# Mixer input stage of a two-layer hybrid decoder step: order of the projections, tiles of the samples' pages, first use of PSUM banks, second key layer

## Chip, cores and metric

The kernel runs on one core of a Trainium2 chip. The metric is the device time of one execution in microseconds (us), lower is better. TensorE (PE) does the matrix products, VectorE (DVE), ScalarE (ACT) and GpSimd (POOL) the element-wise work, SyncE (SP) issues most DMAs; POOL issues the indirect ones. Each engine takes its instructions in one fixed order that the planner wrote down at build time.

## What is computed

The reference runs two layers over 512 prompt tokens and 8 sample tokens (520 columns together). One layer is, cut to what matters here:

```python
x = LN(ALPHA*x + 0.5*swiglu_1(x))
z = x @ w_in                       # u | q | kc vc ks vs kw vw | NSA gates (24) | conv | merge gates
q, ks, kw = rope(q), rope(ks), rope(kw)
kc = gelu(windows(kc_all) @ phi_k1 + pe) @ phi_k2 ; kc = rope(kc)   # the compression branch
vc = gelu(windows(vc_all) @ phi_v1 + pe) @ phi_v2
y_b = g0*attend(q, kc, vc) + g1*attend(q, chosen blocks of ks, vs) + g2*attend(q, kw, vw)   # NSA
x = LN(ALPHA*x + (sig*P_A(s5) + sig*P_B(y_b) + sig*P_C(conv)) @ w_o)
x = LN(ALPHA*x + 0.5*swiglu_2(x))
```

For the 8 samples the rows of `kc`, `vc`, `ks`, `vs` of 2048 past positions lie in pages of 128 rows that a page table names (16 pages of each cache for each sample and layer), and `kw`, `vw` of 512 past positions in a window cache.

## The kernel before, in words

Each large product is done as three products of rounded halves (`mm3`, L239 to L241): 128 weight columns against 264 and then 256 of the 520 token columns, 8 steps of 128 rows, so 48 matmuls for one 128-column block. The weights arrive raw by DMA (`load_raw`, L218, two buffers `raw`) and are split into a rounded part on ACT (L228) and a rest on DVE or POOL (L229) (`split`, four buffers each of `whi` and `wlo`).

`mid` runs the mixers of a layer. It opens PSUM banks (4 `acc`, 2 `aux`, 2 `saT`) and calls `project_kvq`:

- The four blocks of q are computed first, first half of the columns for all four, then the second half, while the norm of the step before delivers its columns block by block (`norm`, L314 to L323).
- Then come kc, vc, ks, vs, kw, vw and the 24 gate columns, in that order, with transposes of finished blocks (`to_rows` L826 and L829, `q_back`, `k_back` L897 and L900) and rope on DVE between them.
- At its start it asks for the 16 compression pages of sample 0 (`fetch_cmp`, L641), for the selection pages of samples 0 and 1 (`fetch_sel`: 32 pages in four tiles of 8 pages, in each tile 3 by indirect DMA of POOL, L1118, and 5 by SP, L1122) and for two window tiles (`fetch_win`, L1127). The planner issues a DMA when its buffer is free, so what SP has queued decides when weights arrive.
- At the end the gates are transposed and spread (L936, L945), after `k_back` of kw.

Then `mid` closes the banks, opens one `saM`, two `saS`, two `cacc`, one `ctp`, and `compress_start` loads and splits the first-layer weights `phi_k1`, `phi_v1` (rest on POOL). `compress_cache` works on one sample at a time: eight steps (`prepare` L688 to L694, `products` L708, 12 matmuls a step, steps alternate between keys and values), then `second`: GELU, the second layer (keys: four matmuls with 64 weight columns each, `w2` and the rotated `w2r`, for two heads, L736; values L740) and the rope of keys (L742 to L744). Keys and values of one sample share a bank, which a matmul of zeros clears first (L702); sample 0 has a bank for each.

`samples` attends for two samples at a time (four groups g). Its scores and values are computed in quarters of the array, 32 columns each: L1189 (selection scores, two banks), L1198 and L1199 (window), L1249 (selection values), L1258 (window values), L1262 to L1264 (own row and compressed values). After the selection values of g it asks for the pages of g+1 into the same four tiles. The groups 0 to 2 are woven with two samples of `compress_cache` each, group 3 with the prompt's attention (`weave` takes the streams' next pieces by costs written in the code; the planner then moves single instructions ahead when it believes them ready).

Of the kernel before, what the change touches and what calls it, by code (L numbers as in the profile page):

```python
# [17 lines left out]
NTOK = 520  # L18
# [104 lines left out]
class Trunk:  # L123
# [36 lines left out]
    def make_consts(self):  # L160
# [7 lines left out]
        zero = c.tile([128, 16], BF, name="zero")  # L168
        nc.vector.memset(zero, 0.0)
        self.zerob = zero[:, 0:1].to_broadcast([128, 128])  # L170
# [329 lines left out]
    def mid(self, l):  # L500
# [16 lines left out]
        self.w2r = a.tile([128, 64], F32, name="w2r")  # L517
        self.hpe = a.tile([128, 2], F32, name="hpe")
        kcv, sag = self.pool(att, "kcv", 2, side="right"), self.pool(att, "sag", 4, side="right")
# [3 lines left out]
        self.open_banks(4, 2)  # L523
# [6 lines left out]
        with ExitStack() as sc, ExitStack() as pb:  # L530
            self.cacc, self.ctp = self.psum(pb, "cacc", 2), self.psum(pb, "ctp", 1)
            cp = self.pool(sc, "cmp")
            with ExitStack() as s0:
                C = self.compress_cache(l, cp, kcv, cx, G, self.compress_start(l, self.pool(s0, "cp")))
# [78 lines left out]
    def page_rows(self):  # L613
# [5 lines left out]
        with self.tc.tile_pool(name="pg", bufs=1) as p:  # L619
            f = p.tile([128, NS, 2, NG], F32, name="f")  # L620
            nc.vector.tensor_copy(f, self.pt.rearrange("p b (z n) -> p b z n", z=2)[:, :, :, :NG])
# [22 lines left out]
    def compress_start(self, l, p):  # L644

        nc, I = self.nc, self.I
        self.w1 = []
        pet = p.tile([128, 2, 2, 8], F32, name="pet")
        for i in range(2):
            raw = self.rawp.tile([128, 8, 256], F32, name="raw")  # L650
            w = raw.rearrange("p k (z h) -> p (k z) h", h=128)
            nc.sync.dma_start(w, I[("nsa_phi_k1", "nsa_phi_v1")[i]][l].rearrange("(q p) h -> p q h", p=128))
            nc.sync.dma_start(self.w2[:, i], I[("nsa_phi_k2", "nsa_phi_v2")[i]][l])
            nc.sync.dma_start(pet[:, i], I[("nsa_pe_k", "nsa_pe_v")[i]][l].rearrange("p (z q) -> p z q", z=2))
# [4 lines left out]
        nc.vector.memset(self.w2r, 0.0)  # L659
        nc.vector.tensor_scalar(self.w2r[:, 0:8], self.w2[:, 0, 8:16], -1.0, None, op0=OP.mult)  # L660
        nc.vector.tensor_copy(self.w2r[:, 8:16], self.w2[:, 0, 0:8])
        return p, pet

    def compress_cache(self, l, p, kcv, cx, G, start):
# [3 lines left out]
        p0, pet = start  # L668
# [5 lines left out]
        def prepare(b, G, s):  # L674

            qq, i = s // 2, s % 2
# [19 lines left out]
        def products(b, acc, s):  # L696
            qq, i = s // 2, s % 2
# [3 lines left out]
            if s == 0 and b:  # L701
                nc.tensor.matmul(acc[0], self.zerob, self.zerob[:, None, :].to_broadcast([128, 4, 128]), start=True,  # L702
                                 stop=False, skip_group_check=True)
            for m, x in enumerate((xh, xh, xl)):
                for q2 in range(2):
                    for z in range(2):
                        w = self.w1[i][z][m == 1]
                        nc.tensor.matmul(o, w[:, 2 * qq + q2, :], x[:, 2 * q2:2 * q2 + 2, z:z + n],  # L708
                                         start=not b and s < 2 and q2 + z + m == 0, stop=s > 5 and q2 == 1 and z == 1 and m == 2,
                                         skip_group_check=True)  # L710

        def second(b, acc):
# [20 lines left out]
            for j, w in enumerate((self.w2[:, 0], self.w2r)):  # L733
                for kv in range(2):
                    r = slice(kv * 64, kv * 64 + 64)
                    nc.tensor.matmul(pa[r, j * 128:j * 128 + 128], w, h[:, kv, :], start=True, stop=True)  # L736
                    if b == 0:
                        nc.tensor.matmul(pa[r, 384 + j * 32:416 + j * 32], w, hp[0][:, 0, kv], start=True, stop=True)
# [1216 lines left out]
```

## Time and profile before

| | us |
|---|---|
| median of 3 runs | 3106.2 (3099.05 to 3106.55) |
| profiled execution, its own time | 3104.94 |
| its span | 3103.2 |
| PE busy | 3028.1 (98%) |
| DVE busy | 1598.7 (52%) |
| ACT busy | 1120.1 (36%) |
| POOL busy | 536.1 (17%) |
| mean granted clock of PE | 0.987 |

The mean granted clock is a share of 2.4 GHz; a stretch with 0.50 runs at 1.2 GHz. Matmuls overlap, so a duration of one (0.28 us) is longer than the distance between two (0.12 us); a stretch's cost is read from starts. Layer 0's `project_kvq` begins about 403 us into the span and layer 1's about 1942 us; the stretch from there to the prompt's attention is the one that the change touches.

### The profile page before, as it was taken

To read this page: it belongs to the slowest core of one execution; us is meant where nothing else is said; L and a number is where in the kernel's file an instruction comes from. 1 tells how busy PE (TensorE), PEld (TensorE's weight loads), DVE (VectorE), ACT (ScalarE), POOL (GpSimd) and SP (SyncE) were. 2 spreads that over 40 slices of the span, in tenths; PEclk is the share of its full clock that TensorE was granted. 3 is DMA by queue.
4 is the path that set the end of the run, shared out by engine and by line. 5 is a ranking of instruction groups with operands and counts; after the bars stand their busy time and mean duration, and the time that the engine had idled before them with its cause. 6 is when DMAs were issued, how large, how long until landed. Compare 5 with 4: busy or idle time off the path is not lost. (4 is left out here: it accounts for less than half of the span.)

```text
span 3103.2 us, 62136 instructions
## 1 busy us (share of the span) xinstructions
PE 3028.1 (98%) x25364; PEld 2906.8 (94%) x25364; DVE 1598.7 (52%) x3586; ACT 1120.1 (36%) x2226; POOL 536.1 (17%) x809
## 2 busy tenths in 40 slices
PE   8999999999999999999999999999999999999998
PEld 8999998777999999999999999887789999999998
DVE  7633356566655365333496333565666453743334
ACT  4332235456224233232233222354652242333322
POOL 2611031321001021001147010213210010210010
PEclk9999999999999999999999999999999999999999
DMA  5543254632553232232234332547234433223221
GB/s 159 198 148 133 89 159 134 209 96 63 156 138 103 88 101 91 82 99 86 82 121 169 96 103 76 172 124 218 83 93 140 122 98 102 89 82 103 89 87 64
DMA packets 358630, 360.17 MB, mean 116 GB/s; under 512 B 40068, under 2 KB 341668, under 8 KB 358216
## 3 DMA queue, kind: packets, MB, share of 16 engines
q1 hardware_dynamic: 342584, 333.58, 34.4%
q0 software_dynamic: 7440, 20.00, 2.2%
q8 instruction: 199, 3.26, 0.4%
q10 hardware_dynamic: 8320, 2.62, 0.4%
q14 instruction: 87, 0.71, 0.1%
HBM read 332.48 MB, written 36.28 MB: 119 GB/s over the span
## 5 line engine op out<-in xcount | busy, mean ns | idle before, releaser
L239 PE MATMUL ps<-xh,whi 128*128 128x264 f32 (+1 forms) x4448 | 1257.6, 285 | 14.1 <-ACT whi L228 6.1
L240 PE MATMUL ps<-xl,whi 128*128 128x264 f32 (+1 forms) x4448 | 1257.4, 284 | 2.0 <-DVE xl L323 2.0
L241 PE MATMUL ps<-xh,wlo 128*128 128x264 f32 (+1 forms) x4448 | 1254.1, 283 | 2.4 <-DVE wlo L229 2.4
L229 DVE TENSOR_TENSOR wlo<-raw,whi 128x1024 fp32r<-128x1024 f32 (+3 forms) x432 | 496.0, 1151 | 741.2 <-ACT whi L228 736.9
L239 PEld LDWEIGHTS ps<-xh,whi 128*128 128x128 f32 x4448 | 837.2, 189 | 18.7 <-ACT whi L228 6.9
L240 PEld LDWEIGHTS ps<-xl,whi 128*128 128x128 f32 x4448 | 839.5, 189 | 3.5 <-DVE xl L323 2.2
L241 PEld LDWEIGHTS ps<-xh,wlo 128*128 128x128 f32 x4448 | 838.5, 189 | 4.1 <-DVE wlo L229 3.6
L228 ACT ACTIVATE whi<-raw 128x1024 fp32r<-128x1024 f32 (+2 forms) x452 | 444.6, 988 | 891.0 <-PE ps L240 776.4
L240 PE MATMUL ps<-hl,whi 128*128 128x256 f32 (+1 forms) x1408 | 398.3, 283 | 0.0
L239 PE MATMUL ps<-hh,whi 128*128 128x256 f32 (+1 forms) x1408 | 398.2, 283 | 0.0
L241 PE MATMUL ps<-hh,wlo 128*128 128x256 f32 (+1 forms) x1408 | 398.1, 283 | 0.0
L241 PEld LDWEIGHTS ps<-hh,wlo 128*128 128x128 f32 x1408 | 265.3, 188 | 0.2
L239 PEld LDWEIGHTS ps<-hh,whi 128*128 128x128 f32 x1408 | 264.9, 188 | 0.3
L240 PEld LDWEIGHTS ps<-hl,whi 128*128 128x128 f32 x1408 | 264.8, 188 | 0.1
L260 POOL TENSOR_TENSOR xf<-xf,shift 128x264 f32<-128x264 f32 (+1 forms) x84 | 79.4, 983 | 1028.6 <-ACT shift L257 1028.6
L384 DVE TENSOR_TENSOR s<-s,ps 128x264 f32<-128x264 f32 (+1 forms) x176 | 74.3, 424 | 277.3 <-PE ps L241 277.0
L708 PE MATMUL ps<-xc,whi 128*128 128x256 f32 (+1 forms) x1024 | 167.4, 297 | 1.0 <-ACT xc L693 0.9
L385 ACT ACTIVATE hh<-s 128x264 fp32r<-128x264 f32 (+1 forms) x176 | 72.7, 415 | 245.2 <-DVE s L384 245.1
L708 PEld LDWEIGHTS ps<-xc,whi 128*128 128x128 f32 x1024 | 142.2, 193 | 14.6 <-issue 7.7
L1118 POOL DMA_INDIRECT sg<-in_selT_dram,idx x96 | 96.2, 1002 | 275.9 <-PE ps L1249 248.7
L382 ACT ACTIVATE s<-ps 128x264 f32<-128x264 f32 (+1 forms) x176 | 66.3, 379 | 128.7 <-PE ps L241 126.5
L386 DVE TENSOR_TENSOR hl<-s,hh 128x264 fp32r<-128x264 f32 (+1 forms) x176 | 76.5, 436 | 33.5 <-ACT hh L385 33.5
(471 smaller groups left out, 4206.8 us busy)
## 6 DMA issues: line engine op xcount, KB each, us to landing
raw<-in_ffn_w_gu_dram SPq DMA_DIRECT2D x86, 1024.0 KB, 5.3
raw<-in_w_in_dram SPq DMA_DIRECT2D x38, 1024.0 KB, 5.4
raw<-in_ffn_w_down_dram SPq DMA_DIRECT2D x32, 1024.0 KB, 4.9
sg<-in_selT_dram SPq DMA_DIRECT2D x160, 128.0 KB, 3.1
cx<-in_cmpT_dram SPq DMA_DIRECT2D x128, 128.0 KB, 2.2
raw<-in_cmpT_dram SPq DMA_DIRECT2D x128, 128.0 KB, 2.5
raw<-in_ffn_w_down_dram SPq DMA_DIRECT2D x16, 768.0 KB, 4.3
W<-in_winT_dram SPq DMA_DIRECT2D x16, 512.0 KB
```

Of the source, the lines that this page charges most:

```text
L228: self.copy = self.nc.scalar.activation(hi, raw, AF.Copy)
L229: self.lo.tensor_sub(lo, raw, hi.bitcast(F32))
L239: nc.tensor.matmul(o, hi[:, k], rh, start=start and k == 0, stop=False)
L240: nc.tensor.matmul(o, hi[:, k], rl, start=False, stop=False)
L241: nc.tensor.matmul(o, lo[:, k], rh, start=False, stop=stop and k == nk - 1)
L260: nc.gpsimd.tensor_sub(self.xf[:, g, a:b], self.xf[:, g, a:b], sc[:, :n])
L382: nc.scalar.activation(s[:, :n], g, AF.Silu)
L384: nc.vector.tensor_mul(s[:, :n], s[:, :n], u)
L385: nc.scalar.activation(hh[:, j, a:b], s[:, :n], AF.Copy)
L386: nc.vector.tensor_sub(hl[:, j, a:b], s[:, :n], hh[:, j, a:b].bitcast(F32))
L708: nc.tensor.matmul(o, w[:, 2 * qq + q2, :], x[:, 2 * q2:2 * q2 + 2, z:z + n], start=not b and s < 2 and q2 + z + m == 0, stop=s > 5 and q2 ...
L1118: nc.gpsimd.indirect_dma_start(out=t[:, k], out_offset=None, in_=flat, in_offset=bass.IndirectOffsetOnAxis(ap=self.idx[:, l, b, z, k:k + 1 ...
```

## The change

- `project_kvq`: the order of the blocks is now q, kc, vc, ks, kw, gates, vs, vw. ks and kw share one raw buffer, vs and vw another, each filled by two DMAs of 128 columns (`kvq_tiles`); the gates' weights have a tile of their own, loaded early. The selection pages' SP DMAs of group 0 are queued behind the loads of all these weights (`rows_in`).
- The gates' transposes and spreading come before the last block; `phi_k1` is loaded and split before vw's product, `phi_v1` after it, rests on DVE (`compress_weights`); small weights come early (`compress_small`). The row outputs leave by POOL's queue.
- One compression bank (`cacc0`) is open during the projections, and `acc` has three banks there, not four.
- `compress_cache` does the four key steps first and then the four value steps; a `start` on the first matmul of each takes the place of the matmul of zeros. The second key layer is one matmul with 128 weight columns (`w2k`, plain and rotated side by side) over both heads; its rope is four multiplies on 64 partitions where two on 128 stood.
- The samples' pages lie in eight tiles of 4 pages; a group's first halves are asked for after half of the selection values of the group before, the second halves after all.
- Each bank of `samples` is opened by a DVE memset of its first column. The own-row and compressed values are ordered so that neighbours use different quarters.

```diff
@@ mid
-        self.open_banks(4, 2)
+        pb = ExitStack()
+        self.banks.close()
+        self.cacc = [self.psum(pb, "cacc0", 1)]
+        self.open_banks(3, 2)
...
-        with ExitStack() as sc, ExitStack() as pb:
-            self.cacc, self.ctp = self.psum(pb, "cacc", 2), self.psum(pb, "ctp", 1)
+        with ExitStack() as sc, pb:
+            self.cacc.append(self.psum(pb, "cacc1", 1))
+            self.ctp = self.psum(pb, "ctp", 1)
@@ compress_start / compress_weights
-            self.lo = nc.gpsimd
-            with self.tc.issue_after(self.queries.ins):
-                self.w1.append([self.split(w[:, 8 * z:8 * z + 8]) for z in range(2)])
-            self.lo = nc.vector
+    def compress_weights(self, l, i):
+        raw = self.rawp.tile([128, 8, 256], F32, name="raw")
+        w = raw.rearrange("p k (z h) -> p (k z) h", h=128)
+        self.nc.sync.dma_start(w, self.I[("nsa_phi_k1", "nsa_phi_v1")[i]][l].rearrange("(q p) h -> p q h", p=128))
+        self.w1.append([self.split(w[:, 8 * z:8 * z + 8]) for z in range(2)])
@@ compress_cache
-            qq, i = s // 2, s % 2
+            i, qq = s // 4, s % 4
...
-            if s == 0 and b:
-                nc.tensor.matmul(acc[0], self.zerob, self.zerob[:, None, :].to_broadcast([128, 4, 128]), start=True,
-                                 stop=False, skip_group_check=True)
...
-                                         start=not b and s < 2 and q2 + z + m == 0, stop=s > 5 and q2 == 1 and z == 1 and m == 2,
+                                         start=qq + q2 + z + m == 0, stop=qq == 3 and q2 == 1 and z == 1 and m == 2,
...
-            for j, w in enumerate((self.w2[:, 0], self.w2r)):
-                for kv in range(2):
-                    r = slice(kv * 64, kv * 64 + 64)
-                    nc.tensor.matmul(pa[r, j * 128:j * 128 + 128], w, h[:, kv, :], start=True, stop=True)
+            nc.tensor.matmul(pa[:, :256].rearrange("p (k n) -> p k n", k=2), self.w2k, h[:, 0:2, :], start=True, stop=True)
...
-            nc.vector.tensor_mul(t, pa[:, 128:256], self.C["kc_sin"])
-            nc.vector.tensor_mul(kcT, pa[:, :128], self.C["kc_cos"])
+            for kv in range(2):
+                r = slice(kv * 64, kv * 64 + 64)
+                nc.vector.tensor_mul(t[r], pa[64:128, kv * 128:kv * 128 + 128], self.C["kc_sin"][r])
+                nc.vector.tensor_mul(kcT[r], pa[0:64, kv * 128:kv * 128 + 128], self.C["kc_cos"][r])
@@ kvq_tiles (new)
+        yield from self.win_tiles(l, 512, 768)
+        for c in (0, 128):
+            if c:
+                yield self.split(self.graw)
+            raw = self.rawp.tile([128, 8, 256], F32, name="raw")
+            for i in range(2):
+                o = 1280 + c + 256 * i
+                self.rows_in = self.nc.sync.dma_start(raw[:, :, 128 * i:128 * i + 128],
+                                                      w[:, o:o + 128].rearrange("(k p) f -> p k f", p=128))
+            for i in range(2):
+                yield self.split(raw[:, :, 128 * i:128 * i + 128])
@@ project_kvq
-        with self.tc.issue_after(self.power.ins):
-            self.fetch_sel(l, sag, 0)
-        self.fetch_win(l, sw, 0)
...
+        w, wsv = next(wt), next(wt)
+        with self.tc.issue_after(self.power.ins), self.tc.issue_after(self.rows_in.ins):
+            self.fetch_sel(l, sag, 0, 0)
+            self.fetch_sel(l, sag, 0, 1)
+        self.fetch_win(l, sw, 0)
         for half, ps in self.proj_halves(w):
...
+        kv_rows(0, sk)
+        q_back()
+        sv = project(wsv)
+        kv_rows(2, wk)
+        k_back(0)
+        gates()
+        self.compress_weights(l, 0)
+        wv = project()
+        kv_rows(1, sv)
         k_back(2)
+        outputs(0)
+        self.compress_weights(l, 1)
+        kv_rows(3, wv)
+        outputs(1)
@@ fetch_sel
+    def fetch_sel(self, l, pg, g, h):
+        for z in range(2):
+            for j in range(2):
+                b, t = 2 * g + j, pg.tile([128, 4, 256], F32, name="sg")
+                n = 2 - h
...
+                for k, s in enumerate(self.pages(src, l, b, 8 * z + 4 * h + n, 4 - n)):
+                    nc.sync.dma_start(t[:, n + k], s)
@@ samples
+    def opened(self, pool):
+        b = self.bank(pool)
+        self.nc.vector.memset(b[:, 0:1], 0.0)
+        return b
...
-        M = self.bank(self.saM)
+        M = self.opened(self.saM)
...
             if c % 4 == 3:
+                if g < 3:
+                    self.fetch_sel(l, pg, g + 1, c // 4)
                 yield 1900.0
-        if g < 3:
-            self.fetch_sel(l, pg, g + 1)
...
         for j in range(2):
-            own, o = slice(32 * j, 32 * j + 32), slice(64 + 32 * j, 96 + 32 * j)
-            nc.tensor.matmul(O[own, :128], sT[:, own], self.srows[:, 128:256], start=False, stop=True, skip_group_check=True)
-            nc.tensor.matmul(O[own, 128:256], sT[:, o], self.srows[:, 384:512], start=False, stop=True, skip_group_check=True)
+            own = slice(32 * j, 32 * j + 32)
             nc.tensor.matmul(O[own, 256:384], pc[:, own], vc[:127, j], start=False, stop=True, skip_group_check=True)
+        for br in range(2):
+            for j in range(2):
+                own, o = (slice(k + 32 * j, k + 32 * j + 32) for k in (0, 64 * br))
+                nc.tensor.matmul(O[own, 128 * br:128 * br + 128], sT[:, o], self.srows[:, 256 * br + 128:256 * br + 256], start=False,
+                                 stop=True, skip_group_check=True)
```

## Rows read from the trace of the kernel before

**Rows 1.** The page's first part: busy us (share of the span) and instructions.
```profile
PE 3028.1 (98%) x25364; PEld 2906.8 (94%) x25364; DVE 1598.7 (52%) x3586; ACT 1120.1 (36%) x2226; POOL 536.1 (17%) x809
```
**Rows 2.** Waits of PE, the whole span: total us, times, longest.
```profile
PE ps L239 <- ACT whi L228: 6.1, 4, 2.5
```
**Rows 3.** PE by stretch: length, PE busy (instructions), granted clock, DMA share, GB/s.
```profile
460.50:463.60 3.10, 1.03 (x7) 1.00 0.24 46
485.50:493.90 8.40, 5.85 (x26) 0.76 0.64 193
493.90:496.60 2.70, 2.70 (x11) 0.50 0.59 187
1999.80:2003.70 3.90, 0.95 (x4) 0.77 0.52 142
2003.70:2008.70 5.00, 5.00 (x23) 0.50 0.04 5
2028.00:2036.40 8.40, 5.73 (x27) 0.78 0.67 201
2036.40:2039.50 3.10, 3.10 (x13) 0.51 0.40 123
```
**Rows 4.** PE's instructions in order: start, length to the last end, instruction [idle before].
```profile
492.09 1.92 PE L1189 MATMUL ps<-sg,QB 128*32 128x512 f32 x2
493.94 0.64 PE L708 MATMUL ps<-xc,whi 128*128 128x324 f32 x1
```
**Rows 5.** SP's DMA issues in order: kw's and vw's weights, and phi_k1.
```profile
454.06 0.40 SPq L218 DMA_DIRECT2D raw<-in_w_in_dram  x1
...
466.45 0.84 SPq L652 DMA_DIRECT2D raw<-in_nsa_phi_k_dram  x1
```
**Rows 6.** DVE's instructions in order, just ahead of kTs L901 of layer 0.
```profile
487.24 2.22 DVE L924 TENSOR_SCALAR gT<-gT 24x520 f32<-24x520 f32 x1
```
**Rows 7.** PE in order, second layer of sample 1, layer 0.
```profile
526.14 0.41 PE L708 MATMUL ps<-xc,wlo 128*128 128x256 f32 x2
526.47 0.44 PE L736 MATMUL ps<-hc,w 128*64 128x128 f32 x4
...
527.06 0.66 PE L740 MATMUL ps<-w,hc 128*128 128x64 f32 x4
```
**Rows 8.** PE in order, end of the values of group 0, layer 0.
```profile
556.42 0.64 PE L1258 MATMUL ps<-W,PT 128*32 128x128 f32 x16
556.99 0.40 PE L1262 MATMUL ps<-srows,sT 8*32 8x128 f32 x2
...
558.76 0.51 PE L708 MATMUL ps<-xc,whi 128*128 128x256 f32 x2
```
**Rows 9.** PE in order, scores of group 3, layer 0.
```profile
672.02 1.92 PE L1189 MATMUL ps<-sg,QB 128*32 128x512 f32 x16
...
674.19 0.65 PE L1198 MATMUL ps<-W,QB 128*32 128x256 f32 x8
```
**Rows 10.** PE's groups by line: operation xcount | busy us, mean ns.
```profile
L702 PE MATMUL ps<-zero 128*128 128x512 bf16 x14 | 5.4, 388 | 0.0
```
**Rows 11.** PE in order, selection scores of group 1, layer 0.
```profile
571.57 1.05 PE L1189 MATMUL ps<-sg,QB 128*32 128x512 f32 x2
...
576.09 1.14 PE L1189 MATMUL ps<-sg,QB 128*32 128x512 f32 x4 [2.02 <-DMA raw<-in_cmpT_dram]
...
577.53 1.06 PE L1189 MATMUL ps<-sg,QB 128*32 128x512 f32 x6
```
**Rows 12.** SP's issues for group 1, the table loads L628, and all engines 555 to 599.3 us.
```profile
554.87 14.38 SPq L1122 DMA_DIRECT2D sg<-in_selT_dram  x20
...
L628 SPq TENSOR_LOAD <-pt x64: 521/972/1108, 409.8 to 2196.6; - x64
...
555.00:599.30 44.30, 41.36 (x377) 33.08 (x377) 22.44 (x71) 21.37 (x45) 12.04 (x12) 1.00 0.70 215
```
**Rows 13.** DVE in order: the last blocks of the norm's first half, layer 0.
```profile
419.58 0.88 DVE L323 SCALAR_TENSOR_TENSOR xl<-xf,lnb,xh 128x264 fp32r<-128x264 f32 x2
```

More of the change, by code (lines that the diff above doesn't have):

```diff
@@ L763, in compress_cache @@
         for b in range(NS):
-            acc = [self.bank(self.cacc) for _ in range(1 if b else 2)]
+            acc = [self.bank(self.cacc[(b + 1) % 2])] if b else [self.bank(c) for c in self.cacc]
             if b + 1 < NS:
@@ L920, in project_kvq, with outputs, gates @@
-        w = next(wt)
+        def outputs(j):
+            k, sv = ("sel", "win")[j], self.srows.rearrange("p (j f) -> p j f", j=2)[:, j]
+            nc.gpsimd.dma_start(O[k + "_p"][l, 0].rearrange("(t p) a h d -> p t (a h d)", p=128), self.rows[:, :, j * 256:j * 256 + 256])
+            dst = O[k + "_s"][l, :, 511] if j else O[k + "_s"][l, :, 0]
+            nc.gpsimd.dma_start(dst.rearrange("b a h d -> b (a h d)"), sv)
+        def gates():
+            tp = self.bank()
+            for t in range(4):
+                nc.tensor.transpose(tp[:, t * 24:t * 24 + 24], self.gT[:, NS + t * 128:NS + t * 128 + 128], self.ident[:24, :24])
+            nc.vector.tensor_copy(self.gtok, tp[:, :96].rearrange("p (t c) -> p t c", t=4))
+            A = p.tile([24, 4, 2, 64], F32, name="gR", tag="sq")
+            for d in range(2):
+                nc.vector.tensor_mul(A[:, :, d].rearrange("p g (j h) -> p g j h", j=2),
+                                     self.gT[:, 0:NS].rearrange("p (g j) -> p g j", j=2)[:, :, :, None].to_broadcast([24, 4, 2, 32]),
+                                     self.C["gA"][:24, None, None, :].to_broadcast([24, 4, 2, 32]))
+            tp = self.bank()
+            for g in range(4):
+                nc.tensor.matmul(tp[:, 3 * g:3 * g + 3], A[:, g].rearrange("p d r -> p (d r)"), self.C["gB"][:24], start=True, stop=True)
+            nc.vector.tensor_copy(self.gat, tp[:, :12].rearrange("p (g r) -> p g r", g=4))
@@ new lines, in project_kvq @@
+        self.compress_small(l)
+        self.w1 = []
+        self.graw = p.tile([128, 8, 24], F32, name="graw")
+        nc.sync.dma_start(self.graw, I["w_in"][l][:, 1792:1816].rearrange("(k p) f -> p k f", p=128))
+        q_rows(0)
+        f = [project()]
+        q_rows(1)
+        f.append(project())
+        q_rows(2)
+        sk = project()
+        raw_rows(0, f[0])
+        q_rows(3)
+        wk = project()
+        raw_rows(1, f[1])
+        q_rope()
+        w, wsv = next(wt), next(wt)
@@ L1186, in samples @@
         for c in range(2):
-            S = self.bank(self.saS)
+            S = self.opened(self.saS)
             for z, j, r in quarters:
-                nc.tensor.matmul(S[r].rearrange("p (n t) -> p n t", n=4), QB[:, 2 * g + j], G[z, j][:, 4 * c:4 * c + 4, 0:128],
+                nc.tensor.matmul(S[r].rearrange("p (n t) -> p n t", n=4), QB[:, 2 * g + j], G[z, j, c][:, :, 0:128],
                                  start=True, stop=True)
@@ L1193, in samples @@
                                     msk[:, 8 * c:8 * c + 8, None].to_broadcast([128, 8, 64]), op=OP.add)
-        S = self.bank(self.saS)
+        S = self.opened(self.saS)
+        for z, j, r in quarters:
+            nc.tensor.matmul(S[r, :256], QB[:, 2 * g + j], G["w", j][:, 256 * z:256 * z + 256], start=True, stop=True)
         for j in range(2):
-            for z in range(2):
-                r = 64 * z + 32 * j
-                nc.tensor.matmul(S[r:r + 32, :256], QB[:, 2 * g + j], G["w", j][:, 256 * z:256 * z + 256], start=True, stop=True)
             nc.tensor.matmul(S[32 * j:32 * j + 32, 256:258], QB[:, 2 * g + j], self.kTs[:, :, 2 * g + j], start=True, stop=True)
@@ L1244, in samples @@
         yield 300.0
[L1246 removed]
+        O = self.opened(self.saS)
         for c in range(8):
             for z, j, r in quarters:
[L1249 removed]
+                nc.tensor.matmul(O[r, :128], PT[:, c, r], G[z, j, c // 4][:, c % 4, 128:256], start=c == 0, stop=z == 1 and c == 7,
                                  skip_group_check=True)
             if c % 4 == 3:
+                if g < 3:
+                    self.fetch_sel(l, pg, g + 1, c // 4)
                 yield 1900.0
[L1253 to L1254 removed]
         for c in range(2):
```

111 lines of the change are left out of this document (31 added, 80 removed).

## The prediction, as it was put on record

> **What bounds the kernel now.** I read the page's first part, then PE's waits, then PE by stretch with its granted clock, and last PE's instructions in order at the places that the change touches. PE is busy 98% of the span, every other engine at most 52% [rows 1]. So the time falls where PE gets fewer or cheaper instructions, where it waits less, or where its clock stays up; work taken from another engine is worth only the PE wait that it caused.
>
> PE's waits are small one by one; what makes them dear is the clock after some of them. One group is the wait for rounded weights: 6.1 us in four, the longest 2.5 [rows 2]. In layer 1 that one fills 1999.8 to 2003.7, and the next 5.0 us run at 0.50, 1.2 GHz for 2.4 [rows 3]. The same wait in layer 0 costs 3.10 - 1.03 = 2.07 us and leaves the clock at 1.00 [rows 3]. Its cause is SP's order: the weights of kw, needed about 460, were issued only at 454.06, behind 20 selection pages [rows 5]. The other group ends the projections: from the last projection to the first compression product 8.40 us pass in either layer, with PE busy under 5.9 and a mean clock of 0.76 to 0.78, and the first products after it still run at half clock [rows 3]. In there PE waits for a small DVE copy (kTs) that stood behind a 2.22 us operation on 24 partitions [rows 6]; and one quarter of a later group's scores, which has nothing beside it, takes 1.85 us alone (492.09 to 493.94) [rows 4].
>
> In the compression and sample stretch PE is busy 41.36 of 44.30 us, with DMA engines at 0.70 [rows 12]: bound by PE at some places, by pages at others.
>
> **The change part by part.**
>
> **Projections.** kw's weights now come with ks's, ahead of the pages. The waits go: 2.07 us in layer 0; in layer 1 3.90 us less the 0.5 that its four matmuls need, 3.4, and half of the 5.0 us at half clock, 2.5 [rows 3]. At the end, gates and k_back move in among the projections, and POOL's splits go, beside which DVE was slow. Of the 8.40 us the work that remains is 5.85 busy less the 1.85 of the lone quarter, so 4.0, less half of the 2.4 us that it ran at half clock: 2.8. I leave 0.7 for one hand-over between engines and take 4.9 off, in each layer. The products after it regain half of 2.70 and of 3.10 us: 1.35 and 1.55 [rows 3]. Layer 0: 2.07 + 4.9 + 1.35 = 8.3; layer 1: 3.4 + 2.5 + 4.9 + 1.55 = 12.4; together 20.7. Next late could be phi_k: it is queued behind the same 20 pages, whose issue takes 14.4 us [rows 12], and four more table loads, but it was issued at 466.45 before [rows 5], will be no later, and is wanted near 487. DVE gets four splits from POOL, at 52% busy [rows 1]. The raw tiles by two DMAs of half rows and the outputs by POOL's queue cost nothing on the path: the weights are early now, and nobody waits for the outputs; if that cover were gone, a late load costs what it did, 2 to 6 us a layer [rows 3].
>
> **Three banks.** The four q blocks run step by step beside the norm, in four banks. With three, 63 matmuls can run before the norm's last block; PE had done about 62 when that block landed near 420 [rows 13]. I put 0.5 us a layer, bounds 0 and 4 (a wait of 1.5 and 5.0 us at half clock [rows 3]).
>
> **No clearing.** 14 matmuls of 512 columns go. They are 0.39 us long [rows 10] but overlap their neighbours; bounds 0 and 0.39, I take 0.2 by the distance of 0.12 us of 256-column products [rows 7]: 2.8 us.
>
> **Second key layer.** Before, from the last product (second of the pair that starts at 526.14, so 526.26) to the value layer at 527.06 are 0.80 us [rows 7]. The new matmul is fp32, two passes of 256 columns; group 3's scores give the pace: four rounds of 512 columns take 1.92 us to the last end, two of 256 take 0.65, so 1536 columns more cost 1.27 us, 0.21 for 256 [rows 9]. With 0.12 to the first pass that is 0.55, so 0.25 saved, 16 times: 4.0 us. Four DVE multiplies for two lie behind PE's next products. The Trainium skill, in "TensorEngine Tiling (Array Packing)", sections Tiling Modes and Performance Considerations, speaks against the edit: 64-column operands run as two independent tiles side by side, up to twice as fast, and one wide operand gives that up. By it the term would be nothing, and the sum 3078; it also says that a switch of tiling drains the array, which fits the slack that I count here. The trace agrees with both halves: eight 128-column passes in two halves take 0.59 us to L740 [rows 7].
>
> **Own-row and compressed values.** Twelve passes in one quarter after another take 556.99 to 558.76, 1.77 us; sixteen passes that fill four quarters take 556.42 to 556.99, 0.14 a round [rows 8]. Six rounds of pairs are 0.86, so 0.91 saved, eight times: 7.3 us.
>
> These three give 14.1. In the groups that wait for pages part of it turns into longer waiting; I take three quarters, 10.6, bounds 0 and 14.1.
>
> **Half tiles.** The scores of group 1 are broken up, 571.57 to 578.59, with a wait of 2.02 [rows 11]; those of group 3 take 1.92 in one piece [rows 9]. With 0.9 of other work between them that is 4.2 us for groups 1 and 2 of each layer, 16.8. First halves are asked for earlier and need half the pages, so the first bank should be whole; the second halves and the window tile come as late as ever. I take a third, 5.6.
>
> **What it adds.** SP reads the page table eight times a group, not four: 4 x 0.97 = 3.9 us [rows 12], ahead of window tile and compression pages. I charge 1 us for each of four groups. The 40 memsets of one column are not in the trace; I charge 1 us in all, bounds 0 and the rival below.
>
> Sum: 20.7 - 1.0 + 10.6 + 5.6 - 4 - 1 = 30.9. From the profiled execution's own 3104.94 (span 3103.2, 1.7 around it) that is 3074; the median, 3106.2, lies 1.3 higher.
>
> **The rivals.**
>
> Pages bound groups 1 and 2. For: DMA share 0.70 over the whole stretch, SP's 20 issues take 14.4 us, and its extra 3.9 [rows 12]. Then half of the 14.1 is lost, and each of four groups pays 2 us: 20.7 - 1 + 7 - 8 = 18.7, 3086.
>
> The end of the projections doesn't close: another evacuation or split takes the place of kTs and the clock drops again. Then only the weights' waits go, 2.07 + 3.4 + 2.5 = 8.0: with the rest 18.2, 3087. Both of these at once: 8 - 1 + 7 - 8 = 6, 3099.
>
> Three banks starve PE and its clock falls: 4 us a layer where I put 0.5: 3081.
>
> Slower: the memsets. Each puts DVE's one queue between a bank and PE, 40 times. If PE stands at each for as long as it stood behind the 2.22 us operation [rows 6], 40 x 2.2 = 88 us are lost; from 30.9 / 40 = 0.77 us each the whole gain is gone, at 1 us it is 3114. Against: DVE is busy 22.44 of the 44.30 us and a bank is free long before it is opened.
>
> **How the numbers follow.** A difference under 0.3%, 9 us, can't be told from none. Forecast 3074: 0.56. Pages bound, 3086: 0.17. The end stays open, 3087: 0.08. Both, 3099: 0.07. Three banks, 3081: 0.06. Slower, 3114: 0.06. Faster by over 0.3% are all but the fourth and the last: 0.87; within 0.07; slower 0.06. Range: low, all bounds in favour, 20.7 + 14.1 + 16.8 = 51.6, 3053; high 3097, which takes in the rivals up to 3087 with 10 us of their own and leaves out the two at 3099 and 3114 and a tail below.
>
> **What would show it.** After the change no wait for rounded weights should stand in the projections, and from the last projection to the first product about 3.5 us should pass at clock 1.00; L702 is gone; from the last product to L740 0.55 us; the twelve passes 0.9 us; group 1's first-bank scores in one piece. Wrong would be: PE waiting for DVE memsets; PE waiting for window tiles longer than now; a half-clock stretch where the projections end; products waiting for phi_v's rests, whose last half can only be split once vw's product frees its buffer.

## The result, and the profile after

| | before | after |
|---|---|---|
| median of six runs each, side by side, us | 3103.38 | 3125.66 |
| ratio, 95% interval | | 1.0074 (1.0051 to 1.0097) |
| the profiled execution's own time, us | 3104.94 | 3132.32 |
| its span, us | 3103.2 | 3130.6 |

The change makes the kernel slower by 0.74%, some 22 us, where 3074 had been forecast. PE is still the engine that bounds it, with a share one point lower than in [rows 1], and DVE has not become busier by that share:

```profile
PE 3034.1 (97%) x25242; PEld 2924.0 (93%) x25242; DVE 1615.9 (52%) x3671; ACT 1121.5 (36%) x2226; POOL 525.9 (17%) x809
```

Where the time went is seen from PE by stretch. The first fence is the kernel before, the second the changed one; in each the lines are layer 0's compression and samples (first to last product), layer 0's attention of the prompt with group 3 beside it, and the same two of layer 1. Columns: start and end, length, then busy us of PE, PEld, DVE, ACT, POOL, the granted clock, DMA share and GB/s.

```profile
493.90:652.40 158.50, 152.55 (x1340) 129.97 (x1340) 86.77 (x282) 82.29 (x187) 29.12 (x30) 0.97 0.53 160
652.40:766.90 114.50, 109.65 (x989) 83.75 (x988) 77.38 (x203) 72.04 (x207) 23.65 (x26) 0.97 0.19 56
2036.40:2191.70 155.30, 150.39 (x1339) 127.36 (x1339) 86.56 (x282) 82.05 (x187) 29.05 (x30) 0.99 0.53 161
2191.70:2306.30 114.60, 109.77 (x989) 83.92 (x988) 76.97 (x202) 71.87 (x208) 23.70 (x26) 0.97 0.20 58
```

```profile
488.90:658.40 169.50, 154.40 (x1299) 133.90 (x1296) 97.11 (x311) 84.03 (x191) 33.27 (x35) 0.92 0.53 161
658.40:780.30 121.90, 112.85 (x982) 87.69 (x982) 79.15 (x211) 73.31 (x209) 22.53 (x25) 0.92 0.17 51
2047.40:2211.40 164.00, 148.96 (x1298) 128.65 (x1296) 97.03 (x311) 83.92 (x191) 33.22 (x35) 0.96 0.55 166
2211.40:2333.30 121.90, 112.85 (x983) 87.68 (x982) 79.13 (x211) 73.33 (x209) 22.59 (x25) 0.92 0.17 50
```

The four stretches take 542.9 us before and 577.3 after, 34.4 more, though PE has some 40 matmuls fewer in each of the sample stretches. In the attention the change touches little, group 3's memsets and the order of some operands; it is 7.4 us longer in either layer, at a clock of 0.92 for 0.97. So the loss is idle time of PE and the lower clock that goes with it, not work. Most of that idle time had next to no counterpart before: products wait for the prepared rows `xc`, and the samples' mask for `mk`. PE's waits over the whole span, first the kernel before, then the changed one (us in total, times, longest):

```profile
PE ps L708 <- ACT xc L693: 0.9, 1, 0.9
```

```profile
PE ps L706 <- ACT xc L694: 8.9, 4, 3.0
PE ps L706 <- DVE xc L695: 8.3, 8, 1.2
PE ps L1212 <- DVE mk L1208: 6.8, 4, 2.9
```

The projections did gain. From the norm's statistics to the first product 85.3 us became 79.9 in layer 0, and 89.1 became 81.6 in layer 1: 12.9 us together. About 1 us a layer of that is transposes that now stand behind the first product (kw's and vw's, 489.88 to 490.56 and 491.72 to 492.07). No wait for rounded weights stands in the projections any more; of the four in [rows 2] two stood there (1.3 and 2.5 us), the others at the start of the span, where one of 1.4 us is left. From the start of the last projection matmul to the first product 0.59 us pass, not 8.49. In their place one new wait stands ahead of the first product in layer 0, at the transposes of q:

```profile
PE ps L876 <- DVE rows L840: 2.8, 1, 2.8
```

The same one is 2.1 us in layer 1.

34.4 us lost and 12.9 gained make 21.5 of the 27.4 between the two spans. Most of the rest lies where nothing was edited: from layer 0's attention to layer 1's norm (766.90 to 1947.24, then 780.30 to 1965.85) it is 5.2 us more, at a granted clock of 0.94 and 0.97 in the first two stretches of 59 us, for 0.97 and 1.00.

The local edits do what the prediction's working says, too. PE's instructions after the window values, group 0 of layer 0 (start, duration of the group, line, shapes, count):

```profile
556.67 0.39 PE L1295 MATMUL ps<-vc,pc 127*32 127x128 f32 x4
556.99 0.62 PE L1299 MATMUL ps<-srows,sT 8*32 8x128 f32 x8
557.55 0.75 PE L706 MATMUL ps<-xc,whi 128*128 128x256 f32 x4
```

The twelve passes take 556.67 to 557.55, 0.88 us, for 1.77 in [rows 8]; 0.86 had been worked out.

### The profile page after: what moved, and what is told of

Same layout as the page of the kernel before. It is cut to its first block, busy times and chain, and to the rows that moved or that the text cites. A ratio compares the mean times of both kernels' runs of the same rounds, so it can differ in the third digit from the quotient of the medians.

```text
span 3130.6 us, 62057 instructions
## 1 busy us (share of the span) xinstructions
PE 3034.1 (97%) x25242; PEld 2924.0 (93%) x25242; DVE 1615.9 (52%) x3671; ACT 1121.5 (36%) x2226; POOL 525.9 (17%) x809
## 5 line engine op out<-in xcount | busy, mean ns | idle before, releaser
L236 PE MATMUL ps<-xh,whi 128*128 128x264 f32 (+2 forms) x4448 | 1258.2, 286 | 11.5 <-ACT whi L203 5.6
L237 PE MATMUL ps<-xl,whi 128*128 128x264 f32 (+2 forms) x4448 | 1259.9, 285 | 2.0 <-DVE xl L320 2.0
L238 PE MATMUL ps<-xh,wlo 128*128 128x264 f32 (+2 forms) x4448 | 1256.0, 284 | 1.8 <-DVE wlo L226 1.8
L226 DVE TENSOR_TENSOR wlo<-raw,whi 128x1024 fp32r<-128x1024 f32 (+1 forms) x438 | 505.1, 1156 | 732.0 <-ACT whi L225 723.4
L236 PEld LDWEIGHTS ps<-xh,whi 128*128 128x128 f32 (+1 forms) x4448 | 838.1, 190 | 16.0 <-ACT whi L203 5.9
L237 PEld LDWEIGHTS ps<-xl,whi 128*128 128x128 f32 (+1 forms) x4448 | 841.0, 189 | 3.7 <-DVE xl L320 2.2
L238 PEld LDWEIGHTS ps<-xh,wlo 128*128 128x128 f32 (+1 forms) x4448 | 840.3, 189 | 3.2 <-DVE wlo L226 2.5
L706 PE MATMUL ps<-xc,whi 128*128 128x256 f32 (+1 forms) x1024 | 176.9, 306 | 17.2 <-ACT xc L694 8.9
```

Source lines behind the costliest of these rows:

```text
L226: self.lo.tensor_sub(lo, raw, hi.bitcast(F32))
L236: nc.tensor.matmul(o, hi[:, k], rh, start=start and k == 0, stop=False)
L237: nc.tensor.matmul(o, hi[:, k], rl, start=False, stop=False)
L238: nc.tensor.matmul(o, lo[:, k], rh, start=False, stop=stop and k == nk - 1)
```

## The experiments

All are variants of the two kernels, compared with the kernel before in the same set. The sets ran on several chips, and on some of them the kernel before takes 3194 to 3205 us instead of 3103 to 3109; what differs there is shown under the first set.

| kernel | median, us | before, us | ratio (95%) |
|---|---|---|---|
| e1 projections alone | 3204.41 | 3202.04 | 1.0008 (0.9996 to 1.0019) |
| e2 changed, no memsets | 3184.09 | 3202.04 | 0.9945 (0.9927 to 0.9963) |
| e3 changed, whole tiles | 3219.01 | 3202.04 | 1.0044 (1.0028 to 1.0060) |
| e4 changed, clearing back | 3201.06 | 3202.04 | 0.9993 (0.9981 to 1.0006) |
| e5 changed kernel | 3198.87 | 3204.95 | 0.9989 (0.9977 to 1.0001) |
| e6 before, with memsets | 3209.14 | 3204.95 | 1.0020 (1.0009 to 1.0030) |
| e7 as e2 | 3182.83 | 3204.95 | 0.9942 (0.9929 to 0.9955) |
| e8 as e1 | 3202.78 | 3204.95 | 1.0002 (0.9993 to 1.0011) |
| e9 before, plain DMAs | 3100.84 | 3105.69 | 0.9983 (0.9972 to 0.9994) |
| e10 changed, plain DMAs | 3124.12 | 3105.69 | 1.0056 (1.0043 to 1.0068) |
| e11 as e10, no memsets | 3102.82 | 3105.69 | 0.9992 (0.9980 to 1.0004) |
| e12 projections alone, plain DMAs | 3097.24 | 3105.69 | 0.9968 (0.9957 to 0.9979) |
| e13 as e12, values' order | 3100.54 | 3109.30 | 0.9975 (0.9962 to 0.9988) |
| e14 as e12, key layer | 3107.10 | 3109.30 | 0.9995 (0.9985 to 1.0004) |
| e15 as e12, no clearing | 3104.06 | 3109.30 | 0.9982 (0.9970 to 0.9994) |
| e16 as e12, half tiles | 3091.07 | 3109.30 | 0.9947 (0.9929 to 0.9964) |
| e17 as e10, M's memsets alone | 3105.70 | 3193.50 | 0.9711 (0.9689 to 0.9733) |
| e18 as e10, the other memsets alone | 3123.89 | 3193.50 | 0.9772 (0.9751 to 0.9792) |

**First set: one part of the changed kernel undone (e2 to e4), or all but the projections (e1).** The edits: e2 and e7 drop the memset; e3 puts `fetch_sel` of before back; e4 puts the clearing back (sample 0 keeps keys first); e1 and e8 undo all of these, and the key layer, the order of values and that of the window scores.

```diff
     def opened(self, pool):          # e2, e7
         b = self.bank(pool)
-        self.nc.vector.memset(b[:, 0:1], 0.0)
         return b
...
-                b, t = 2 * g + j, pg.tile([128, 4, 256], F32, name="sg")     # e3
+            b, t = 2 * g + j, pg.tile([128, 8, 256], F32, name="sg")
...
-            i, qq = s // 4, s % 4                                            # e4
+            i, qq = (s % 2, s // 2) if b else (s // 4, s % 4)
+            if s == 0 and b:
+                nc.tensor.matmul(acc[0], self.zerob, ..., start=True, stop=False, skip_group_check=True)
...
-            nc.tensor.matmul(pa[:, :256]..., self.w2k, h[:, 0:2, :], start=True, stop=True)   # e1, e8, with all above
+            for j, w in enumerate((self.w2[:, 0], self.w2r)): ...
```

> The changed kernel with everything behind the projections as before: plain banks, 8-page tiles, the matmul of zeros and the alternating steps, the two-matmul second key layer, the old order of own-row, compressed and window operands. Left of the change: the projections' order, early weights, three acc banks, pages queued behind the weights. If the projections gain by themselves what the traces show at their end (5.4 us in layer 0, 7.5 in layer 1), it takes 3103 - 13 = 3090, at the forecast of this part 3083, and the rest of the change costs 35 us. If pages queued behind the weights are what makes the sample stage late, the gain is eaten there and it takes 3103 or more.

> The changed kernel with its 40 memsets of a bank's first column left out. Theory: they cost little, since the trace shows PE waiting for one only twice, 1.6 us in all: 3121 to 3126. Rival, that they hold DVE's order and through it the clock: the loss against before goes, 3105 or less.

> The changed kernel with whole 8-page tiles, asked for after all selection values, four table reads on SP for a group instead of eight. If late pages (SP's longer queue) cause the loss: 3105 to 3112. If the order of the products and the clock cause it whatever the tiles: 3126 or, with the broken scores back, up to 3134.

> The changed kernel with the 14 matmuls of zeros and with key and value steps alternating again (samples 1 to 7; sample 0 keeps keys first, as phi_v comes late). If the order of the steps, four key steps and then four value steps, is what puts products that wait for pages ahead of window scores: 3108 to 3115. If not: the 14 matmuls come back, 3126 to 3130.

Without its memsets the changed kernel is faster than the kernel before, by 0.55%: the first sign that the memsets are not small. But the yardstick was another one than in the result, 3202 us. The reason stands in ACT's instructions of any of these runs; here e5's, around POOL's batch of gathers for group 1 (issued from 561.0 to 577.6), then its windows before and in the batch, and then the first kernel after in a batch of its own:

```profile
561.93 0.73 ACT L694 ACTIVATE xc<-raw 128x256 fp32r<-128x256 f32 x2 [1.48 <-PE ps L706]
572.82 0.72 ACT L694 ACTIVATE xc<-raw 128x256 fp32r<-128x256 f32 x2 [10.16 <-remote]
...
553.00:561.00 8.00, 6.35 (x74) 5.54 (x74) 6.04 (x23) 5.57 (x13) 0.00 (x1) 1.00 0.33 99
562.70:572.70 10.00, 5.34 (x54) 2.99 (x46) 0.53 (x2) 0.00 (x0) 6.30 (x7) 0.76 0.64 191
```

```profile
553.60:563.60 10.00, 9.88 (x118) 8.72 (x118) 4.46 (x13) 4.94 (x10) 7.75 (x8) 1.00 0.76 231
```

In 10 us of the batch ACT does nothing and DVE 0.53 us, and the release has no event in the trace ("remote"); on the chip of the result ACT and DVE work on through the same batch. There are eight batches, and standstills of this size are of the order of the 99 us between 3202 and 3103. They are not the same for all kernels: with half tiles a group's twelve gathers come as eight and four, and in six of e5's batches ACT stands for 10.0 to 10.2 us; with whole tiles they come in one go, and in half the batches of e1 and e6 it stands for 15.6. So in these sets the changed kernel has an advantage that it has not elsewhere.

**Second set: the yardstick, and the memsets by themselves.** e5 is the changed kernel unedited, e6 the kernel before with `opened` in `samples` in place of `bank`.

```diff
-        M = self.bank(self.saM)      # e6; the same for two S and one O
+        M = self.opened(self.saM)
```

> The changed kernel itself, as the yardstick of this set, since the first four experiments ran where the kernel before takes 3202 us, not 3103. If the comparison doesn't hang on that, 1.007 of the kernel before again. If DVE and ACT standing still during POOL's gathers, which the first four experiments show, changes it: nearer to 1.00.

> The kernel before with nothing but the 40 memsets of a bank's first column. Theory memsets: they alone cost what the changed kernel lost, 20 to 40 us, 1.006 to 1.013 of before, most of it where group 3 runs beside the attention (PE waits for M's memset behind DVE's rope operations, and the clock drops). Rival, that the order of products and pages did it: 1.000 to 1.002.

> The changed kernel without its memsets, once more beside the changed kernel. Theory memsets: 20 to 40 us faster than the changed kernel, so 0.994 to 1.001 of before. Rival: within 5 us of the changed kernel.

> The projections' part of the change alone, once more beside the changed kernel. By the traces of before and after at the projections' end it is worth 13 us: 0.996 of before. By what it gave in the first set, 1.000 to 1.002: a gain that is lost again in the sample stage, with pages later.

On this chip the changed kernel is level with the kernel before, whose whole tiles make it stand still for longer. The same 40 memsets cost 0.0047 in the changed kernel (e5 against e7), 15 us, but 0.0020 in the kernel before, 6 us. So they have no one price that could be added.

**Third set: the gathers taken away.** POOL reads page numbers and issues plain DMAs in both kernels.

```diff
-                nc.gpsimd.indirect_dma_start(out=t[:, k], out_offset=None, in_=flat, in_offset=...)
+            for k, s in enumerate(self.pages(src, l, b, 8 * z, NG, mybir.EngineType.Pool)):
+                nc.gpsimd.dma_start(t[:, k], s)
```

> The kernel before, with POOL's gathers (12 for a group, of a page each by a list of rows) replaced by plain DMAs on POOL's queue whose page number POOL reads from the table. It takes away what makes ACT and DVE stand still for 10 to 13 us in each of eight batches in the last two sets (8 x 12 = 96 us). If the gathers do that: about 3105, 0.97 of before, as the time of the kernel before in the first comparison. If plain DMAs of POOL hold the engines as well: 3200.

> The changed kernel with the same plain DMAs in place of the gathers. If the standstill was all that set the sets apart, the loss of the first comparison comes back: 1.007 of the kernel before with plain DMAs, 3126. If the loss was of another kind: 0.999 of it, 3101.

> The changed kernel with plain DMAs and without its 40 memsets. Theory memsets and clock: 20 us or more faster than with them (15 to 16 us with gathers), at or below the kernel before with plain DMAs. Rival, order of products and late pages: within 5 us of the one with memsets.

> The projections' part of the change alone, with plain DMAs. Theory: its 13 us, seen in the traces of before and after at the projections' end, show now: 3092, 0.996 of the kernel before with plain DMAs. Rival, that pages queued behind the weights give them back: 1.000 of it or more.

This set ran where the kernel before takes 3106, so e9 says only that plain DMAs cost nothing there (0.9983). That they take the standstill away where it occurs is shown by e17 and e18, which ran where before takes 3193.5 and came to 3106 and 3124. e10 repeats the result: 23.3 us more than e9. e11 gives the main part of the cause: without memsets 21.3 us less, level with before. The waits for `xc` are not the memsets' doing, though: e11 still has 7.6 us on ACT and 6.8 on DVE. The projections alone (e12) give 3.6 us, not 13. In its trace they do give 13.7 (82.4 and 82.2 us for 88.6 and 89.7 in e9's), but 6.2 us are lost ahead of them (see e16), and layer 1's sample stage is 6.9 us longer (159.3 for 152.4), layer 0's 0.5 shorter.

**Fourth set: one part at a time on top of e12.** The edits are those of the change itself, with the rest of e12 untouched.

```diff
+            for br in range(2):                       # e13, own rows; the window scores go by quarters too
+                for j in range(2): ...                # neighbours in different quarters
...
+            nc.tensor.matmul(pa[:, :256]..., self.w2k, h[:, 0:2, :], start=True, stop=True)      # e14
...
+            i, qq = s // 4, s % 4                     # e15, and no matmul of zeros
...
+                b, t = 2 * g + j, pg.tile([128, 4, 256], F32, name="sg")                         # e16
```

> The projections alone with plain DMAs (3097, 0.997 of before), plus the new order of own-row, compressed and window operands. The forecast's term: 7.3 us less, at three quarters 5.5: 3091, 0.995. Rival, the sample stage waits for window tiles and pages in any case: within 3 us of 3097.

> The projections alone with plain DMAs (3097), plus the second key layer as one operand with its rope in four multiplies. The forecast's term: 4.0 us less: 3093. By the Trainium skill's page TensorEngine Tiling (Array Packing), by which two 64-column halves run side by side: 0, 3097. Rival, the four multiplies of 64 partitions delay DVE: slower, 3100.

> The projections alone with plain DMAs (3097), plus four key steps ahead of four value steps in samples 1 to 7 and no matmuls of zeros. The forecast's term: 2.8 us less, 3094. Rival, the other order of steps asks for the second raw tile's half of the pages no later but leaves PE behind products that wait: 3100 or more.

> The projections alone with plain DMAs (3097), plus pages in half tiles, with eight reads of the page table on SP for a group. The forecast's terms: 5.6 less for whole scores, 4 more for SP: 3095. Rival, SP's reads and the later window tile make the stage wait: 3101 to 3107.

Against e12's 0.9968 they are +2 us (e13), +8.4 (e14), +4.3 (e15) and -6.5 (e16), each give or take 4 to 6 us (95%). Added up from e12 they give 0.9995, and e11, which has them all, is at 0.9992: within this noise the parts add.

e14's trace shows what eats the key layer's gain. PE at the second key layer of sample 3, with the products behind it, first e12 and then e14:

```profile
570.33 0.44 PE L738 MATMUL ps<-hc,w 128*64 128x128 f32 x4
570.60 0.39 PE L738 MATMUL ps<-hc,w2r 128*64 128x128 f32 x4
...
571.39 0.49 PE L710 MATMUL ps<-xc,whi 128*128 128x256 f32 x2
```

```profile
572.42 0.60 PE L737 MATMUL ps<-hc,w2k 128*128 128x256 f32 x2
...
573.21 0.48 PE L711 MATMUL ps<-xc,whi 128*128 128x256 f32 x2
```

From the first key pass to the next product it was 1.06 us and is 0.79, 0.27 less for the 0.25 of the forecast. The Trainium skill's "TensorEngine Tiling (Array Packing)", section Tiling Modes, has different tiles working in parallel. The trace of before agrees: at the place of [rows 7] the passes of the two halves start 0.01 us apart (526.47 and 526.48), and their rounds 0.11 apart where in the changed kernel a joined pass of twice the columns takes 0.21 (521.42 to 521.63). The two forms are not level all the same; the difference lies where the form changes (0.21 us for 0.12 from the last product to the first key pass, the rest ahead of the value layer). DVE in the same place, e12 and e14:

```profile
571.62 0.29 DVE L744 TENSOR_TENSOR kct<-ps,cst 128x128 f32<-128x128 f32 x1 [2.40 <-PE ps L742]
...
572.02 0.68 DVE L696 TENSOR_TENSOR xc<-cx,xc 128x512 fp32r<-128x512 f32 x1
```

```profile
573.44 0.29 DVE L745 TENSOR_TENSOR kct<-ps,cst 64x128 f32<-64x128 f32 x1 [2.06 <-PE ps L739]
...
574.35 0.28 DVE L746 TENSOR_TENSOR kcT<-ps,cst 64x128 f32<-64x128 f32 x1
574.67 0.69 DVE L697 TENSOR_TENSOR xc<-cx,xc 128x512 fp32r<-128x512 f32 x1
```

A multiply on 64 partitions takes as long as one on 128 (0.29 us), so the rest `xc`, for which the next products wait, begins 1.23 us after the first multiply instead of 0.40. In e14 PE waits for it, in e12 not at all; layer 0's sample stage of e14:

```profile
PE ps L711 <- DVE xc L697: 2.2, 4, 1.2
```

It is as much in layer 1: 4.5 us in all, about the 4.3 that PE saved (16 times 0.27). That takes the gain away; the 8.4 us, give or take 4.5, are not all accounted for. Between these two executions the sample stages differ by 3.4 us in layer 0 and by -2.8 in layer 1.

e13's shorter values do not show in its time. PE waits longer at the window scores; in layer 1, e12 and then e13 (us, times, longest):

```profile
PE ps L1231 <- issue: 3.3, 2, 2.0
```

```profile
PE ps L1229 <- issue: 4.2, 2, 2.5
```

In layer 0 the same wait goes from 0.2 to 1.8 us. Both layers together that is 2.5 us more, of the 7.3 saved. The trace names nothing that ends these waits ("issue"); of the two window tiles that the last of them could be for, one had landed at 2155.9, 5.4 us before PE went on at 2161.29, so a wait for the tiles is not shown. In this pair of executions e13's sample stages are 4.1 us shorter together, and the attentions, with group 3 beside them, 3.0 longer; its 2 us, give or take 5, leave room for anything from -3 to +7. from -3 to +7.

e16's gain lies elsewhere than where it was looked for. e1, e3, e8 and e12 to e15 all have a stall in layer 0's first feed-forward, some 270 us ahead of the projections; e16 has not, nor have the kernels before and after. The waits of e12 between 128 and 145, and the windows of e12 and e16:

```profile
PE ps L239 <- ACT whi L228: 2.4, 1, 2.4
PE ps L241 <- DVE wlo L229: 1.5, 1, 1.5
...
132.00:145.00 13.00, 9.11 (x64) 8.47 (x62) 11.14 (x15) 7.73 (x16) 12.29 (x20) 0.74 0.45 146
```

```profile
132.00:145.00 13.00, 13.00 (x121) 12.63 (x120) 6.57 (x11) 3.34 (x9) 8.28 (x31) 1.00 0.43 150
```

It costs 3.9 us of idle PE and a quarter of 9.11 at the lower clock, 6.3 us together: as much as e16 gains. So without it the projections would be worth about 3.6 + 6.3 = 10 us, and half tiles about nothing where gathers stop nobody. The planner writes one order for the whole program, and whole tiles together with the new projections gave another one there. What tipped it is open; the one edit with instructions ahead of the stall is that half tiles pick their page numbers in three copies at 19 us, not one. In the first set e3 loses 0.0055, 17.6 us, against e5; the same stall is 6.3 of that, and a longer standstill with whole tiles can be the rest.

**Fifth set: which memsets.** Both are e10 with part of its memsets.

```diff
-        self.nc.vector.memset(b[:, 0:1], 0.0)           # e17, in opened
+        nc.vector.memset(M[:, 0:1], 0.0)                # e17, in samples
...
-        M = self.opened(self.saM)                       # e18
+        M = self.bank(self.saM)
```

> The changed kernel with plain DMAs and with the 8 memsets of the one M bank alone. With all 40 memsets it is 1.0056 of before, with none 0.9992. If the wait seen beside the attention (M's memset behind DVE's rope operations, then half clock) is the cost: 1.003 to 1.006. If it is the memsets of the score and value banks: 1.000.

> The same with the other 32 memsets alone, those of the score banks and the value bank. By the theory that M's cost the time: 0.999 to 1.002. If these do: 1.004 to 1.006. If both cost about half, the two together give the 0.0064 between all and none; if each alone costs as much as both, it is the drop of the clock after either that counts.

e18 is at e10's time (3123.89 and 3124.12), e17 near e11's (3105.70 and 3102.82). The theory that M's memset costs the time falls, though its two waits of 0.8 us are the only ones that stand for a memset in the changed kernel's trace. In e18 there is no wait for a memset to be seen; there is this one, layer 0's attention, e17 and then e18:

```profile
PE ps L1052 <- DVE cP L1048: 0.3, 1, 0.3
```

```profile
PE ps L1052 <- DVE cP L1048: 2.9, 2, 2.6
```

DVE on the way to `cP`, first e17, then e18 (start, duration, line, shapes):

```profile
687.41 0.41 DVE L1043 TENSOR_REDUCE cm<-cP 128x8 f32<-128x256 f32 x1
687.74 0.67 DVE L995 TENSOR_TENSOR raw<-qT,raw 64x512 fp32r<-64x512 f32 x1
...
689.62 0.69 DVE L996 TENSOR_TENSOR raw<-qT,raw 64x512 fp32r<-64x512 f32 x1
690.34 0.17 DVE L1047 TENSOR_TENSOR cm<-cm,gtok 128x8 f32<-128x8 f32 x1
...
691.02 0.41 DVE L1048 TENSOR_TENSOR cP<-cP,cm 128x256 f32<-128x256 f32 x1
```

```profile
686.17 0.67 DVE L995 TENSOR_TENSOR raw<-qT,raw 64x512 fp32r<-64x512 f32 x1
688.14 0.42 DVE L1078 TENSOR_REDUCE pm<-ps 128x1 f32<-128x256 f32 x1 [1.30 <-PE ps L1077]
...
688.73 0.69 DVE L996 TENSOR_TENSOR raw<-qT,raw 64x512 fp32r<-64x512 f32 x1
...
689.59 0.41 DVE L1043 TENSOR_REDUCE cm<-cP 128x8 f32<-128x256 f32 x1
690.03 0.69 DVE L995 TENSOR_TENSOR raw<-qT,raw 64x512 fp32r<-64x512 f32 x1
...
691.83 1.12 DVE L1047 TENSOR_TENSOR cm<-cm,gtok 128x8 f32<-128x8 f32 x1
692.98 0.69 DVE L996 TENSOR_TENSOR raw<-qT,raw 64x512 fp32r<-64x512 f32 x1
693.70 0.43 DVE L1048 TENSOR_TENSOR cP<-cP,cm 128x256 f32<-128x256 f32 x1
```

The order is another one. The waits are those of the pair with all memsets and with none: e10 has e18's line to the digit, e11 has e17's. In e18 the reduction L1043 stands behind a pair of L995 and L996 and behind L1078, for which DVE idles 1.30 us waiting for PE, and another such pair stands ahead of L1048. The memsets take 0.06 us each; what the planner put around them costs 2.6 us of PE, and then the clock. Leaving memsets out, the 199 DVE instructions of each layer's attention stand in one and the same order in the changed kernel, e10 and e18, and in one other order in e11 and e17, and the time goes with the order: from the last compression product to the attention's last product 120.5 to 120.6 us a layer in the first three, 113.7 to 114.8 in the other two. That makes the order the cause as far as these runs can tell; none has e18's order without the memsets. Group 3 beside the attention, layers 0 and 1, e17 and e18:

```profile
655.10:704.80 49.70, 45.52 (x392) 34.27 (x393) 33.72 (x114) 29.82 (x96) 7.74 (x13) 0.86 0.24 73
2194.20:2242.80 48.60, 44.19 (x393) 33.12 (x392) 33.56 (x114) 29.83 (x96) 7.74 (x13) 0.89 0.25 77
```

```profile
653.70:709.10 55.40, 47.90 (x392) 36.90 (x393) 34.23 (x117) 29.97 (x96) 7.68 (x13) 0.82 0.21 64
2203.50:2258.80 55.30, 47.79 (x392) 36.79 (x392) 34.17 (x117) 29.84 (x95) 7.68 (x13) 0.81 0.21 65
```

That is 12.4 of the 18.1 us between the two spans. The other 5.7 lie in pieces of 3 us and less on either side, and two runs of e17 differ by up to 10.6. Of the 29.7 us between e10's span and e11's the attentions make 13.7. The sample stages make 13.6, where DVE's order is the same in both (they differ by 0.3 between e17 and e18), and the cause of that part is open.

## Why the prediction was wrong, point by point

| term | forecast, us | measured, us |
|---|---|---|
| projections with three banks | -19.7 | -3.6; about -10 without a stall that came elsewhere |
| no clearing | -2.8, three quarters counted | +4.3 (e15); -1 (e4 against e5) |
| second key layer | -4.0, three quarters counted | +8.4 |
| own-row and compressed values | -7.3, three quarters counted | +2 |
| half tiles and SP's reads | -1.6 | -6.5, of which 6.3 is that stall's absence |
| memsets | +1 | +21.3 |

The measured ones come to +26 us; the changed kernel with plain DMAs is at +23.3.

**The memsets** are the step that failed by most. "I charge 1 us in all" was right for the waits: 1.6 us in two. The rival that was named, PE standing behind each memset in DVE's queue, is not what happened either: 0.06 us each, and no wait at those of the score and value banks. What failed is the rule behind both, that an instruction costs what it takes or what waits for it. In this program it also costs what the written order becomes: 12 to 14 of the 21 us are shown to go with DVE's order in the attentions. The price is 21 us in one kernel, 15 on another chip, 6 in the kernel before.

**Second key layer.** PE's 0.25 us a sample came as worked out [rows 7]. The step that failed is "Four DVE multiplies for two lie behind PE's next products". They lie ahead of the rests that those products read, half the partitions don't halve their time, and 4.5 us of new waits take the gain away. Why it is 8.4 us slower, and not level, is open.

**Values.** The 0.9 us a group came (0.88 for 1.77), and the time did not follow: +2 us in e13, give or take 5. The step that failed is the three quarters of it that were counted. 2.5 us came back as longer waits at the window scores, the place that the rival of late pages points to, but the trace does not show that they are for pages; where the rest went is open.

**Projections.** The weights' waits went as forecast, and the end closed better than forecast, to 0.59 us. Of the 20.7 us, 17.8 were forecast for the stretch up to the first product (the other 2.9 for the products behind it), and 12.9 came there: a new wait of 2.8 and 2.1 us stands at q's transposes. DVE's copy of the rows is behind rests of the next weights there (two of 1.2 us from 469.38, the copy at 471.66), and in layer 1 the clock drops with it (0.60 from 2030 to 2036): the rival of "another evacuation", in the middle and not at the end. Three banks cost nothing that could be seen; the waits of the norm's blocks are not longer.

**No clearing.** Two comparisons disagree in sign, each within about 5 us of none; the 2.8 us are not seen, and what the other order of steps does is not settled. **Half tiles.** Group 1's first-bank scores have no wait and no product among them now, only small matmuls of the compressed branch (570.32 to 574.56, for 7.0 us in [rows 11]); the time of the stage did not follow. What SP's reads cost was not taken apart.

The signs named came (no wait for rounded weights in the projections, a closed end, L702 gone, 0.55 us from a sample's last product to the value layer, twelve passes in 0.9 us, group 1's scores but for small matmuls in one piece), and the kernel was slower all the same: each looked at an edited place, and the loss was at others. Of the wrong signs one came, faintly: PE waiting for a memset.

e16, the projections with half tiles and plain DMAs and the rest as before, is faster than both kernels: 0.9947 (0.9929 to 0.9964) of the kernel before.

## What to carry to other kernels

Where a planner writes one fixed order for all engines, 40 added instructions of 0.06 us each can cost 20 us, and part of it at other instructions: price an edit as a draw of a new order too, and leave out those that buy little. After a run lay PE's two traces against each other from the start of the span, before a gain or a loss is credited to the edit; here 6 us of one part's "gain" were a stall some 270 us ahead of it. Work taken off PE does not have to show in the time: in e13 0.9 us a group went, and no gain is to be seen.

## What was not expected of the hardware

- On chips where the kernel before takes 3194 to 3205 us, ACT and DVE stand still for 10 us while POOL issues eight gathers (15.6 in half the batches of twelve in e1 and e6), and PE works 5.34 of 10 us; on others they work on. With plain DMAs from POOL's queue e18 takes on the first kind what e10 takes on the second, 3124 us.
- A DVE multiply of 64 partitions by 128 takes 0.29 us, one of 128 partitions the same.
- In fp32 one operand of 128 columns over 256 is 0.27 us shorter than four of 64 columns over 128, counted to the next product.
